# A decoder trunk on one Trainium2 core: the first stage's seven-product chunk set six units later, with its sums, its block fetches, the constants and the position terms moved

## The chip, the cores and the metric

The kernel runs on one core of one Trainium2 chip. The metric is the device time of one execution in microseconds (us), a median over several executions. PE is the matrix engine, DVE the vector engine, ACT the scalar engine, POOL the GpSimd engine and SP the sync engine, which here does nothing but issue DMAs. The page of the profile gives line numbers of kernel.py; L145 is a helper that records every call on PE, DVE and ACT, so rows are told apart by the names of their tiles, not by their lines.

## What is computed

Two layers of a decoder on 256 tokens of width 1024, all in float32. The change lies in the first half-step feed-forward block of layer 0, the first thing that the kernel does:

```python
def swiglu(x, w_gate, w_up, w_down):
    return (jax.nn.silu(x @ w_gate) * (x @ w_up)) @ w_down

# layer 0, first sub-layer; D_MODEL 1024, D_FF 2816, 256 tokens
hdn = swiglu(rmsnorm(x, ng[0]), ffn1_w_gate[0], ffn1_w_up[0], ffn1_w_down[0])
x = x + 0.5 * rmsnorm(hdn, ng[1])
```

The layer's mixer, which comes next, uses `compress_blocks`: blocks of 32 keys (or values), each with a position vector `pe` added, are multiplied by a weight `w1`. Since `(k + pe) @ w1` is `k @ w1` plus a term without tokens in it, the kernel works that constant term out once, ahead of the mixer. These are the position terms of the title.

```python
blk = k[:, idx] + pe[None, None, :, None, :]
return jax.nn.silu(blk.reshape(...) @ w1) @ w2
```

## The kernel before, in words

**Products in three parts.** Every weight is split into a high part `whi` (ACT casts it) and a low part `wlo` (DVE subtracts the high part from the raw weight), and the activations likewise into `xth` and `xtl`. One product is three matmuls: high by high, high by low, low by high. Each has a result of 128 tokens by 512 columns.

**Units.** The stage `f10` (`ffn`, L600, with `first=True`) streams its weights as units of 512 KB, a tile of 128 x 1024. They are counted here from 0, as the code counts them. Units 0 to 31 are four chunks of hidden columns (chunks 0, 1, 2 and 4 of 512 columns, eight units each, gate and up side by side). Units 32 to 35 are the last 256 columns, and units 36 to 49 are rows of the down weights. `unit` (L308) fetches a unit into a tile `raw` (a pool of 4 buffers), lets ACT write `whi` and DVE write `wlo`, and takes the buffers for these from two rings of six and four. `work` (L812) does the matmuls of one unit for one half of the tokens, t = 0 or t = 1: six matmuls for each. `lagged` (L565) runs over the units, t = 0 at once and t = 1 some units later, and calls what is registered for a unit: `at` ahead of it, `groups` behind it.

**Chunk ends.** After eight units the gate and up results of a token half stand in two PSUM banks. `chunk_end` (L607) multiplies: ACT writes silu of the gate into `sg`, DVE multiplies it by the up result, PE transposes it into `tp`, ACT and DVE split it into `hth` and `htl`. Only these reads by ACT and DVE free the two banks. The tiles `acc` share six banks.

**Seven products.** Hidden chunk 3 is computed by seven block products in place of eight (a scheme of Strassen's kind). `sums` (L674) first builds sums of the activation blocks in a tile `hx` (DVE), splits them into `sumh` and `suml` (ACT and DVE), and after that `hx` is free. The chunk's weight blocks come as eight transfers of 512 KB. Four go into a tile `wa` that is kept: `blocks` (L687) fetches two of them through SP at each of two units. Two are streamed through `raw` in phase one, which DVE also adds onto `wa`; two are streamed in phase six and added as well. The remaining sums of blocks are made by transfers that POOL issues and that accumulate onto `wa` in memory (`gather`, L699), four in number here. `wide_phases` (L758) gives the seven phases and a close, each run behind a given unit. A phase has twelve matmuls.

**Constants and position terms.** `tables` (L936) fetches two tables of 414 and 320 KB. `constants` (L942) fetches four small ones (`pv`, `pc`, `mu`, `small`). `compress_bias` (L963) fetches 1 MB of weights `cw`, multiplies them by the position vectors (four DVE operations of 128 x 512), adds them up in halves (ten DVE operations) and ends with two small matmuls into `tp` and a DVE operation that writes `cbias`.

**What sets the order.** A table, `GROUPS` (L38), says behind which unit each of these steps is recorded. Its row `False` serves this stage alone: `sums` at unit 7, blocks at units 13 and 14, phases behind units 16, 17, 18, 20, 21, 22, 23 and the close behind 24; the sums for the down weights at 30, the blocks of the down weights at 31 and 33. The tables are recorded at unit 11, the constants at 14, the position terms at units 24 to 33, in `wa[:, 0]`. The framework's scheduler then fixes the order on each engine, and each engine works through its own list in that order; SP's and POOL's transfers wait in their lists too. So a row that waits holds up all rows behind it on its engine.

Of the kernel before, what the change touches and what calls it, by code (L numbers as in the profile page):

```python
# [11 lines left out]
F32 = mybir.dt.float32  # L12
# [24 lines left out]
SEVEN = {True: (3, 4), False: (3,)}  # L37
GROUPS = {  # L38
    True: {"sums": 7, "down": 26, 3: (5, 6, (8, 9, 10, 12, 13, 14, 15, 16)), 4: (14, 16, (18, 19, 20, 22, 23, 24, 25, 26)), 0: (25, 26, (32, 33, 34, 35, 36, 37, 38))},
    False: {"sums": 7, "down": 30, 3: (13, 14, (16, 17, 18, 20, 21, 22, 23, 24)), 0: (31, 33, (39, 40, 41, 42, 43, 44, 45))},  # L40
}


# [133 lines left out]
class _Plan:  # L177
# [27 lines left out]
    def add(self, gen):  # L205
        self.strands.append(_Strand(gen))
# [16 lines left out]
class _Trunk:  # L223
# [376 lines left out]
    def ffn(self, units, gpost, last, kind, ahead=(), after=None, first=False, scale=None, following=None):  # L600

        nc, tc = self.nc, self.tc
# [251 lines left out]
        def lag(r):  # L854
            return min(LAG - 2 * (r == LAG - 1) - (LAG <= r < n - 8), max(8 - r if r < 8 else BASE, r + GROW - n))
# [4 lines left out]
        with tc.tile_pool(name="hp", bufs=1, reuse_waits="tile") as hp, self.work_pool():  # L860
            space = lambda dt: hp.tile([P, 2, 10, S], dt, name="hx", tag="hx")
            wa = hp.tile([P, 2, 2, D], F32, name="wa")
            at = {29: [], **({} if first else self.entry(self.scale_of(scale)))}
            add = lambda r, f: at.setdefault(r, []).append(f)
            between = {}
            for c in SEVEN[wide]:
                between.update(zip(groups[c][2], ([f] for f in wide_phases(c))))
            between.update(zip(groups[0][2], ([f] for f in down_phases())))
            add(groups["sums"], sums)
            add(groups["down"], down_sums)  # L870
            if first:
                self.begin(units, work, wa[:, 1].rearrange("p a b -> p (a b)")[:, 0:D])
                for r, f in ((4, lambda: self.stats_first(0)), (5, lambda: self.stats_first(1)), (11, self.tables), (14, self.constants),
                             *zip(range(24, 34), self.compress_bias(wa[:, 0]))):
                    add(r, f)
                pend = self.lagged(units, work, at, early, blocks, between, 3)
            else:
                pend = self.lagged(units, work, at, (lambda r: max(lag(r), r - n + 8)) if kind == "plain" else lag, blocks, between)
            rest = [lambda p=p: work(1, *p) for p in pend[:-2]]
            rest += [lambda p=p, h=h: work(1, *p, (h,)) for h in range(2) for p in pend[-2:]]  # L880
            if kind in ("mixer", "plain"):

                self.nc.scalar.activation(self.sm.tile([P, 2], F32, name="one", tag="st")[:, 0:1], htl[5].bitcast(F32)[:, 0, S - 1:S], AF.Exp)
            if kind in ("mixer", "plain"):
                self.rowsp = self.xp.tile([P, 2, D], F32, name="rows", tag="x8")
                for j, i in enumerate((gpost, last)[:1 if kind == "mixer" else 2]):
                    self.fetch(self.rowsp[:, j], self.rows[i].partition_broadcast(P), self.loads[-4])
                rows = [self.rowsp[:, j] for j in range(2)]
            else:
                row = self.xp.tile([P, 2, D], F32, name="rows", tag="x8")[:, 0]  # L890
                self.fetch(row, self.rows[gpost].partition_broadcast(P), self.loads[-4])
                rows = [row, None]
            self.finish(lambda t: [st[t, "y", 0], st[t, "y", 1]], rest, rows[0], True, kind, 2, ahead, rows[1], after, following)
# [69 lines left out]
    def compress_bias(self, w):  # L963

        nc = self.nc
        self.cbias = self.cp.tile([P, 1], F32, name="cbias")
        tile = []

        def load():
            tile.append(w.rearrange("p s (j e) -> p s j e", e=64))  # L970
            self.fetch(tile[0], self.cw[:, 0:2048].rearrange("p (s j e) -> p s j e", s=2, e=64), self.loads[-1])

        def scale(i, h):
            w = tile[0][:, i, 8 * h:8 * h + 8]
            o = 76 + 16 * i + 8 * h
            nc.vector.tensor_mul(w, w, self.pvt[:, o:o + 8, None].to_broadcast([P, 8, 64]))

        def add(i, n):
            w = tile[0][:, i]
            nc.vector.tensor_add(w[:, 0:n], w[:, 0:n], w[:, n:2 * n])  # L980

        def close():
            tp = self.tpp.tile([P, 4, P], F32, name="tp", tag="tp")
            for i in range(2):
                add(i, 1)
                nc.tensor.matmul(tp[64 * i:64 * i + 64, 0, 0:1], tile[0][:, i, 0], self.tabt[:, 767:768], start=True, stop=True)
            nc.vector.tensor_scalar(self.cbias, tp[:, 0, 0:1], 0.5, None, op0=ALU.mult)

        steps = [lambda i=i, h=h: scale(i, h) for i in range(2) for h in range(2)]
        return [load, *steps, *(lambda i=i: add(i, 8) for i in range(2)), lambda: (add(0, 4), add(1, 4)), lambda: (add(0, 2), add(1, 2)), close]  # L990
# [2011 lines left out]
```

## Time and profile before

| what | us |
|---|---|
| median of 3 runs | 1121.72 (1118.56 to 1121.87) |
| the profiled execution's own time | 1124.68 |
| its span, first to last instruction | 1122.9 |
| what lies around the span | 1.8 |
| PE busy in the span | 1100.0 (98%) |

The span is what every time on the page and in the trace counts from. A row of the timeline gives an instruction's start, its length, what it writes and reads, and in brackets how long its engine had been idle before it and what ended that. The granted clock is the share of full speed at which PE was run. The matmuls are pipelined: one shows 0.39 us, and the next starts 0.23 us behind it.

### The profile page before, as it was taken

What the parts mean: (1) busy time and instruction counts of PE and PEld (TensorE: products, weight loads), DVE (VectorE), ACT (ScalarE), POOL (GpSimd) and SP (SyncE); (2) the same over time, 40 slices, a digit from 0 to 9 for tenths busy, and PEclk for the clock granted to TensorE, in tenths of its full rate; (3) what the DMA queues carried; (4) which work ended last, traced back from release to release, by engine and by line L of the source; (5) the groups of instructions that cost most, each with busy time, mean ns of one, the idle gap of its engine ahead of it and who ended that gap; (6) DMA issues with size and microseconds to landing.
All of it is one profiled execution on the core that took longest, in us unless ns stands there. A gap on an engine that the chain in (4) does not pass through costs nothing.

```text
span 1122.9 us, 17815 instructions
## 1 busy us (share of the span) xinstructions
PE 1100.0 (98%) x6687; PEld 931.8 (83%) x6687; DVE 954.7 (85%) x1521; ACT 681.5 (61%) x1135; POOL 70.5 (6%) x122
## 2 busy tenths in 40 slices
PE   8999999999999999999999999999999999999997
PEld 6787888898988788888888888899989987888885
DVE  6878869889889999798898798886898798997985
ACT  5664656559866577665576666458514445775662
POOL 0010010000000011100010101000300000111000
PEclk9899999999999999999999999999999999999999
DMA  7877687453335588886668877732332324878870
GB/s 281 275 181 253 204 205 245 136 191 107 98 119 188 200 248 265 251 251 190 221 193 278 215 276 195 275 147 76 132 117 79 114 114 178 227 261 224 285 195 37
DMA packets 60854, 216.80 MB, mean 193 GB/s; under 512 B 7392, under 2 KB 7392, under 8 KB 60640
## 3 DMA queue, kind: packets, MB, share of 16 engines
q1 hardware_dynamic: 50400, 177.92, 45.6%
q0 software_dynamic: 10368, 37.75, 15.3%
q8 instruction: 52, 0.85, 0.3%
q14 instruction: 34, 0.28, 0.1%
HBM read 214.60 MB, written 1.05 MB: 192 GB/s over the span
## 4 chain that ended last, share of the span: by engine, by line
PE 81%; DVE 9%; ACT 4%; DMA 4%; issue 1%; SPq 0%; DVEq 0%; ACTq 0%
PE acc L145 77%; PE tp L145 4%; DMA raw<-in_wst_dram 4%; DVE wlo L145 3%; ACT whi L145 1%; DVE tm L145 1%; DVE tt L145 1%; DVE xtl L145 1%; ACT xth L145 1%; ACT junk L145 1%; ACT aT L145 0%; SPq L294 0%; ACT lc L145 0%; DVE x L145 0%; DMA xg<-in_x_dram 0%
## 5 line engine op out<-in xcount | busy, mean ns | idle before, releaser
L145 ACT CAST whi<-raw 128x1024 fp32r<-128x1024 f32 x239 | 246.4, 1054 | 123.5 <-DMA raw<-in_wst_dram 77.5
L145 DVE TENSOR_TENSOR wlo<-raw,whi 128x1024 fp32r<-128x1024 f32 x239 | 286.3, 1220 | 26.2 <-ACT whi L145 25.5
L145 PE MATMUL acc<-wlo,xth 128*128 128x512 f32 (+1 forms) x476 | 184.7, 391 | 1.0 <-DVE wlo L145 1.0
L145 PE MATMUL acc<-whi,xth 128*128 128x512 f32 (+1 forms) x476 | 180.3, 396 | 5.3 <-ACT sg L145 3.1
L145 PE MATMUL acc<-whi,xtl 128*128 128x512 f32 (+1 forms) x476 | 184.5, 391 | 0.4 <-DVE xtl L145 0.4
L145 ACT CAST whi<-wa 128x1024 fp32r<-128x1024 f32 (+1 forms) x112 | 115.2, 1044 | 68.3 <-DMA wa<-in_wst_dram 39.5
L145 DVE TENSOR_TENSOR wlo<-wa,whi 128x1024 fp32r<-128x1024 f32 (+1 forms) x112 | 133.5, 1209 | 19.0 <-ACT whi L145 18.9
L145 PEld LDWEIGHTS acc<-whi,xth 128*128 128x128 f32 x476 | 90.2, 190 | 25.3 <-ACT sg L145 4.3
L145 PEld LDWEIGHTS acc<-wlo,xth 128*128 128x128 f32 x476 | 90.1, 190 | 19.8 <-DVE wlo L145 2.5
L145 PEld LDWEIGHTS acc<-whi,xtl 128*128 128x128 f32 x476 | 90.3, 190 | 19.0 <-DVE xtl L145 0.9
L145 PE MATMUL acc<-whi,hx 128*128 128x512 f32 x320 | 104.2, 391 | 0.0
L145 PE MATMUL acc<-whi,xt 128*128 128x512 f32 x272 | 85.7, 391 | 0.0
L145 DVE TENSOR_TENSOR wa<-wa,raw 128x1024 f32<-128x1024 f32 x44 | 53.8, 1222 | 24.9 <-DMA raw<-in_wst_dram 22.3
L699 POOL DMA_DIRECT2D wa<-in_wst_dram x44 | 38.6, 877 | 555.0 <-DVE wlo L145 537.3
L145 PEld LDWEIGHTS acc<-whi,hx 128*128 128x128 f32 x320 | 60.0, 188 | 12.2
L145 PE MATMUL acc<-whi,sumh 128*128 128x512 f32 x176 | 69.3, 394 | 0.0
L145 PE MATMUL acc<-whi,suml 128*128 128x512 f32 x176 | 68.7, 390 | 0.0
L145 PE MATMUL acc<-wlo,sumh 128*128 128x512 f32 x176 | 68.6, 390 | 0.0
L145 PE MATMUL acc<-wlo,hx 128*128 128x512 f32 x160 | 62.5, 391 | 0.4 <-DVE wlo L145 0.4
L145 PEld LDWEIGHTS acc<-whi,xt 128*128 128x128 f32 x272 | 51.1, 188 | 10.5
L145 PE MATMUL acc<-wlo,xt 128*128 128x512 f32 x136 | 53.4, 393 | 0.2 <-DVE wlo L145 0.2
L145 PE MATMUL acc<-xnh,whi 128*128 128x256 f32 x160 | 46.3, 289 | 0.0
(436 smaller groups left out, 2213.6 us busy)
## 6 DMA issues: line engine op xcount, KB each, us to landing
raw<-in_wst_dram SPq DMA_DIRECT2D x256, 512.0 KB, 4.7
wa<-in_wst_dram POOLq DMA_DIRECT2D x72, 512.0 KB, 6.7
wa<-in_wst_dram SPq DMA_DIRECT2D x17, 512.0 KB, 7.0
lw<-in_wst_dram SPq DMA_DIRECT2D x12, 512.0 KB, 3.5
whi<-in_wst_dram SPq DMA_DIRECT2D x8, 512.0 KB, 5.8
wlo<-in_wst_dram SPq DMA_DIRECT2D x8, 512.0 KB, 5.0
wr<-in_wst_dram SPq DMA_DIRECT2D x8, 512.0 KB, 5.1
grow<-in_rows_dram SPq DMA_DIRECT2D x6, 512.0 KB, 5.7
```

Of the source, the lines that this page charges most:

```text
L145: r = f(out, *a, **k)
L699: nc.gpsimd.dma_start(home(i, p), place[key], accum_op=ALU.add)
```

## The change

Three edits, all for the stage `f10`:

1. In `GROUPS`, row `False`: the sums of chunk 3 are recorded at unit 14 in place of 7; its block fetches at units 18 and 19 in place of 13 and 14; its phases behind units 22, 23, 24, 26, 27, 28, 30 and the close behind 31. The sums for the down weights move from unit 30 to 32, and the second pair of the down weights' blocks from 33 to 32. The phases of the down weights stay.
2. The tables are recorded at unit 14 in place of 11, the constants at 16 in place of 14.
3. The position terms get a tile of their own, the first part of a new `hx` (the tile that the sums of chunk 3 had, and that the later results of the stage take), in place of `wa[:, 0]`, and are recorded at units 19 and 21 to 29 in place of 24 to 33. Their four multiplications are pinned: each has to stay behind the DVE operation recorded just before it.

```diff
@@ -37,7 +37,7 @@
-    False: {"sums": 7, "down": 30, 3: (13, 14, (16, 17, 18, 20, 21, 22, 23, 24)), 0: (31, 33, (39, 40, 41, 42, 43, 44, 45))},
+    False: {"sums": 14, "down": 32, 3: (18, 19, (22, 23, 24, 26, 27, 28, 30, 31)), 0: (31, 32, (39, 40, 41, 42, 43, 44, 45))},
@@ -870,8 +870,8 @@
-                for r, f in ((4, lambda: self.stats_first(0)), (5, lambda: self.stats_first(1)), (11, self.tables), (14, self.constants),
-                             *zip(range(24, 34), self.compress_bias(wa[:, 0]))):
+                for r, f in ((4, lambda: self.stats_first(0)), (5, lambda: self.stats_first(1)), (14, self.tables), (16, self.constants),
+                             *zip((19, 21, 22, 23, 24, 25, 26, 27, 28, 29), self.compress_bias(lambda: space(F32)[:, :, 0:4].rearrange("p s a b -> p s (a b)")))):
@@ -967,11 +967,12 @@
-            tile.append(w.rearrange("p s (j e) -> p s j e", e=64))
+            tile.append(w().rearrange("p s (j e) -> p s j e", e=64))
...
         def scale(i, h):
             w = tile[0][:, i, 8 * h:8 * h + 8]
+            nc.vector.pin = True
```

What this does to the lists of the engines. First place: SP, from unit 10 of the stage on. Before, `raw_415` is unit 10, `raw_437`, `raw_455` and `raw_473` are units 11 to 13 and `raw_512` is unit 14; `wa` are blocks of chunk 3.

```order
L294 DMA raw_415<-in_wst_dram 128x1024
L294 DMA tabs_433<-in_tabs_dram 128x828
L294 DMA tb_434<-in_tabs_dram 128x641
L294 DMA raw_437<-in_wst_dram 128x1024
L294 DMA raw_455<-in_wst_dram 128x1024
L294 DMA raw_473<-in_wst_dram 128x1024
L294 DMA wa_94<-in_wst_dram 128x1024 x2
L294 DMA pv_493<-in_pv_dram 128x108
L294 DMA pc_494<-in_pv_dram 128x32
L294 DMA mu_496<-in_pv_dram 128x48
L294 DMA small_495<-in_rows_dram 128x32
L294 DMA raw_512<-in_wst_dram 128x1024
```

The same place after, where `raw_402` is unit 10, `raw_456` unit 13, `raw_491` unit 14 and `raw_509` unit 15:

```order
L294 DMA raw_402<-in_wst_dram 128x1024
L294 DMA raw_420<-in_wst_dram 128x1024
L294 DMA raw_438<-in_wst_dram 128x1024
L294 DMA raw_456<-in_wst_dram 128x1024
L294 DMA tabs_487<-in_tabs_dram 128x828
L294 DMA tb_488<-in_tabs_dram 128x641
L294 DMA raw_491<-in_wst_dram 128x1024
L294 DMA raw_509<-in_wst_dram 128x1024
L294 DMA pv_539<-in_pv_dram 128x108
L294 DMA pc_540<-in_pv_dram 128x32
L294 DMA mu_542<-in_pv_dram 128x48
L294 DMA small_541<-in_rows_dram 128x32
```

Unit 14 now stands behind the two tables only; the four constants come behind unit 15, and the blocks `wa` behind units 18 and 19. The weights `cw` of the position terms come behind unit 21, where before they came behind unit 27.

Second place: DVE where the position terms are multiplied (`pv` holds the position vectors). Before, `wlo_913`, `wlo_954` and `wlo_975` are units 24 to 26.

```order
L145 TENSOR_TENSOR wlo_913<-raw_910,whi_912 128x1024
L145 TENSOR_TENSOR wlo_954<-raw_951,whi_953 128x1024
L145 TENSOR_TENSOR wa_94<-wa_94,pv_493 128x512 x4
L145 TENSOR_TENSOR formx_1049<-hth_547,htl_548 128x1024
L145 TENSOR_TENSOR wlo_975<-raw_972,whi_974 128x1024
```

After, where `wlo_672` and `wlo_691` are units 21 and 22 and `sg_521` is the product that ends chunk 1 for t = 0:

```order
L145 TENSOR_TENSOR wlo_672<-raw_669,whi_671 128x1024
L145 SCALAR_TENSOR_TENSOR sg_521<-acc_359,rs_y_242,sg_521 128x512
L145 TENSOR_TENSOR hx_628<-hx_628,pv_539 128x512 x2
L145 TENSOR_TENSOR hx_628<-hx_628 128x512
L145 TENSOR_TENSOR hx_628<-hx_628 128x256
L145 TENSOR_TENSOR wlo_691<-raw_688,whi_690 128x1024
```

Two of the four multiplications now stand ahead of unit 22; the other two stand further back, one at a time, between the subtractions of units 22 and 24.

Third place: DVE around phase six of chunk 3, whose two streamed blocks are added onto `wa`. Before, these are `raw_824` and `raw_837`; `wlo_727` is unit 20 and `wlo_768` unit 21.

```order
L145 TENSOR_TENSOR wlo_727<-raw_724,whi_726 128x1024
L145 TENSOR_TENSOR wlo_743<-wa_94,whi_742 128x1024
L145 TENSOR_TENSOR htl_548<-tp_549,hth_547 128x4x128
L145 TENSOR_TENSOR wlo_753<-wa_94,whi_752 128x1024
L145 TENSOR_TENSOR wa_94<-wa_94,raw_824 128x1024
L145 TENSOR_TENSOR htl_548<-tp_585,hth_547 128x4x128
L145 TENSOR_TENSOR wa_94<-wa_94,raw_837 128x1024
L145 TENSOR_TENSOR wlo_768<-raw_765,whi_767 128x1024
```

After, where the blocks are `raw_970` and `raw_983`, `wlo_869` is unit 26, `wlo_912` unit 27, and `sg_812` the product that ends chunk 2 for t = 1:

```order
L145 TENSOR_TENSOR wlo_869<-raw_866,whi_868 128x1024
L145 TENSOR_TENSOR wlo_885<-wa_94,whi_884 128x1024
L145 SCALAR_TENSOR_TENSOR sg_749<-acc_565,rs_y_242,sg_749 128x512
L145 TENSOR_TENSOR wa_94<-wa_94,raw_970 128x1024
L145 TENSOR_TENSOR wlo_895<-wa_94,whi_894 128x1024
L145 TENSOR_TENSOR wa_94<-wa_94,raw_983 128x1024
L145 SCALAR_TENSOR_TENSOR sg_812<-acc_601,rs_y_271,sg_812 128x512
L145 TENSOR_TENSOR wlo_912<-raw_909,whi_911 128x1024
```

A chunk's end, `sg_812`, now stands behind the addition of `raw_983`; before, the chunk ends nearest to these additions stood ahead of both. On PE the first matmuls for t = 1 of unit 8 now come behind the first matmul of unit 13, where before they came behind all of units 8 to 14 for t = 0. Behind this stage the lists of all engines are the same as before.

## The prediction

> **What bounds the kernel now.** I read the page first, then PE's busy time in stretches of 10 us over the stage that the change touches, then the timelines and the chain of waits around the two stretches that stand out. The page:
>
> ```profile
> span 1122.9 us, 17815 instructions
> ...
> PE 1100.0 (98%) x6687; PEld 931.8 (83%) x6687; DVE 954.7 (85%) x1521; ACT 681.5 (61%) x1135; POOL 70.5 (6%) x122
> ...
> PE 81%; DVE 9%; ACT 4%; DMA 4%; issue 1%; SPq 0%; DVEq 0%; ACTq 0%
> ```
>
> PE is busy for 98% of the span and carries most of the chain. The change adds and takes away no matmul, so it can only win PE's pauses, or make new ones. In stretches (columns: PE, PEld, DVE, ACT, POOL busy and count, granted clock, DMA share, GB/s):
>
> ```profile
> 30.00:40.00 10.00, 10.00 (x46) 8.29 (x45) 9.19 (x23) 6.51 (x11) 0.00 (x0) 1.00 0.81 266
> 40.00:50.00 10.00, 7.64 (x21) 5.00 (x21) 6.74 (x15) 6.42 (x7) 0.00 (x0) 0.71 0.82 313
> ...
> 100.00:110.00 10.00, 7.52 (x34) 5.90 (x33) 10.00 (x13) 4.98 (x7) 0.00 (x0) 1.00 0.41 112
> ```
>
> A full stretch starts about 46 matmuls. From 40 to 50 us there are 21, from 100 to 110 us 34. The first stretch also ran at a reduced clock; cut at the clock's own steps:
>
> ```profile
> 40.72:44.13 3.41, 1.70 (x7) 0.79 (x6) 1.78 (x6) 1.39 (x2) 0.00 (x0) 1.00 1.03 420
> 44.13:50.95 6.82, 6.17 (x15) 4.38 (x14) 5.28 (x8) 5.02 (x6) 0.00 (x0) 0.50 0.69 248
> ```
>
> PE's timeline at the first place. Between the first two rows lie 30 starts without a gap, 6.80 / 30 = 0.227 us each; then come three gaps, in the brackets:
>
> ```profile
> 33.93 0.39 PE L145 MATMUL acc<-whi,xtl 128*128 128x512 f32 x1
> ...
> 40.73 0.39 PE L145 MATMUL acc<-whi,xtl 128*128 128x512 f32 x1
> 42.30 0.73 PE L145 MATMUL acc<-whi,xth 128*128 128x512 f32 x2 [1.18 <-ACT whi L145]
> 43.56 0.50 PE L145 MATMUL acc<-wlo,xth 128*128 128x512 f32 x1 [0.53 <-DVE wlo L145]
> ...
> 45.82 0.80 PE L145 MATMUL acc<-whi,xth 128*128 128x512 f32 x1 [0.65 <-ACT sg L145]
> ```
>
> And at the second place one:
>
> ```profile
> 100.36 0.39 PE L145 MATMUL acc<-whi,xtl 128*128 128x512 f32 x1
> 103.23 0.50 PE L145 MATMUL acc<-whi,xth 128*128 128x512 f32 x1 [2.48 <-ACT sg L145]
> ```
>
> The chain of waits tells what lies behind each (start, length, what):
>
> ```profile
> 34.27 6.85 DMA raw<-in_wst_dram
> ...
> 41.20 1.05 ACT whi L145
> ...
> 42.28 1.23 DVE wlo L145
> ...
> 45.08 0.70 ACT sg L145
> ...
> 68.67 10.59 DMA raw<-in_wst_dram
> ...
> 94.77 6.68 DMA raw<-in_wst_dram
> ...
> 101.54 1.04 ACT whi L145
> 102.59 0.60 ACT sg L145
> ```
>
> At 34.27 SP issues unit 14; its cast is also what the first silu (`sg` at 45.08) stands behind on ACT, and PE needs that silu to get a bank back. At 94.77 it is one of the units behind the weights of the position terms, and again a silu stands behind its cast.
>
> **The first pause: 5.4 us, and what the change takes from it.** Gaps: 1.18 + 0.53 + 0.65 = 2.36 us. In the 6.82 us at clock 0.50 PE was busy for 6.17, of which half, 3.1 us, is lost. Together 5.4 us. Why unit 14 was late, on SP and DVE:
>
> ```profile
> 25.25 4.40 SPq L294 DMA_DIRECT2D raw<-in_wst_dram  x3
> 29.69 0.90 SPq L294 DMA_DIRECT2D wa<-in_wst_dram  x2
> ...
> 32.27 1.23 SPq L294 DMA_DIRECT2D mu<-in_pv_dram  x1
> 33.54 0.64 SPq L294 DMA_DIRECT2D small<-in_rows_dram  x1
> 34.27 0.48 SPq L294 DMA_DIRECT2D raw<-in_wst_dram  x1
> ```
>
> ```profile
> 21.83 1.22 DVE L145 TENSOR_TENSOR hx<-xth,xtl 128x1024 f32<-128x1024 f32 x1
> ...
> 26.93 1.22 DVE L145 TENSOR_TENSOR hx<-xth,xtl 128x1024 f32<-128x1024 f32 x1
> 28.07 1.22 DVE L145 TENSOR_TENSOR wlo<-raw,whi 128x1024 fp32r<-128x1024 f32 x1
> 29.53 1.23 DVE L145 TENSOR_TENSOR wlo<-raw,whi 128x1024 fp32r<-128x1024 f32 x1 [0.24 <-ACT whi L145]
> ```
>
> The last row is the subtraction of unit 10. It ends at 30.76 and frees the raw buffer that unit 14 takes. SP could have issued then; instead it worked through two blocks and four constants until 34.2, and the 1 MB of blocks also went ahead of unit 14 on the wire. In the changed list only the two tables stand between, 0.5 us each on SP, and they are out before 30.76. So unit 14 is issued by 30.8 at the latest. It may be earlier, by up to 2 us: unit 10 lands without the tables beside it, and of the sums' additions ahead of unit 9 one of about 1.1 us and one of 0.6 us are gone (the 21.83 and 26.93 rows are two, of which one now stands ahead of unit 8). Time to landing: 6.85 us from the row above as the worst, and in a quiet stretch of the same stage (110 to 140 us) this answer for `raw`:
>
> ```profile
> DMA to landing us min/median/max: 3.7/4.4/5.3
> ```
>
> Landing therefore lies between 28.8 + 4.4 = 33.2 and 30.8 + 6.85 = 37.65; I take 34.5, nearer to the quiet rows since there is only one unit and the tables on the wire. Behind it on ACT come the cast (1.05), a table load and the silu (0.70). The load, in ACT's timeline:
>
> ```profile
> 43.78 1.28 ACT L145 ACT_TABLE_LOAD   x1 [1.53 <-DVE rs_y L145]
> ```
>
> Before it stood 1.53 us for `rs_y`, which DVE finished behind unit 14's subtraction; in the changed list the `rs_y` of t = 0 is finished ahead of that subtraction, so this wait goes. The silu then ends about 3.1 us behind the landing, at 37.6 (36.3 to 40.8). PE wants its bank after the first of unit 13's six matmuls for t = 0. Those six end at 41.12 now (42.30 less 1.18); five of them at 0.227 make 1.1 us, so PE asks at 40.0. Margin 2.4 us, cost 0 to 0.8 us; I take 0. A gain below nothing is excluded here, since PE runs without a gap from 12 to 41 us and its matmuls stay. The 5.4 us are gone.
>
> **What the moved transfers cost.** Units 11 to 22, four blocks of `wa`, the 1 MB of `cw` and the tables are 12 x 0.52 + 4 x 0.52 + 1.05 + 0.75 = 10.2 MB from 24 us on. At 266 GB/s (the 30 to 40 row) they take 38 us and are in by 62; at the 420 GB/s of the 40.72 row 24 us, by 48. PE needs unit 22 after 131 matmuls and 16 transposes, at 40.0 + 131 x 0.227 + 16 x 0.11 = 71.5 (0.44 us for four transposes is a quarter more than three matmul starts, by the difference of starts around them). Even the slow end leaves 9 us for cast, subtraction and the position terms ahead of it on DVE. I take no pause. `cw` waits on SP for the sums' last subtraction, since it takes their `hx`: that ends, by the list, one subtraction behind unit 17's, near 46 us, while SP's next issue, unit 22, waits for unit 18's buffer until about 48. So it holds nothing up.
>
> **The second pause: 2.48 us.** DVE and SP behind it:
>
> ```profile
> 91.43 0.33 SPq L294 DMA_DIRECT2D wa<-in_cw_dram  x1
> 93.52 1.57 SPq L294 DMA_DIRECT2D raw<-in_wst_dram  x2
> ```
>
> ```profile
> 99.07 2.50 DVE L145 TENSOR_TENSOR wa<-wa,pv 128x512 f32<-128x512 f32 x4 [4.33 <-DMA wa<-in_cw_dram]
> ```
>
> `cw` went ahead of two units, and DVE stood 4.33 us for it with the subtractions of later units behind it. In the changed lists nothing of the position terms is left here. At their new place DVE may stand for `cw` as well: from 46.3, at 91.43 to 99.07 = 7.6 us, it is in at 53.9, and DVE gets there (behind unit 21 and `sg_521`) at about 54.7. Cost 0; if DVE stands 4.33 again, unit 22 is ready near 62 against 71.5, still 0. So 2.48 us are won.
>
> **The new place that is tight.** Unit 26 takes the ring buffer of phase one's first block, which PE leaves at 75.5 by the same count; with cast and subtraction (1.05 + 1.22) it frees a raw buffer at 77.8, and `raw_983` is issued. The addition (1.2) and `sg_812` (0.75) stand behind its landing. PE transposes `sg_812` after 209 matmuls and 20 transposes, at 89.6. With 4.4 us to land, `sg_812` is ready at 84.2; with the 10.59 us of the same transfer before (the 68.67 row; POOL's accumulating transfers ran beside it) at 90.3, 0.7 us late. I take 0, with 0.7 as the upper end. The rest of the chunk's waits were hidden before and keep their spacing from phase one to six.
>
> **Edits at nothing.** POOL no longer waits for the position terms, which now stand elsewhere:
>
> ```profile
> 142.09 1.19 POOL L696 DMA_DIRECT2D wa<-in_wst_dram  x2 [57.21 <-DVE cbias L145]
> ```
>
> PE had no gap there, so the wait cost nothing and its end brings nothing. The later sums for the down weights have the stretch of units 32 to 40 for cover, 20 us and more. Behind the stage all lists are the same; PE gets there earlier, and the transfers follow it since they wait for buffers that PE frees.
>
> **The sum.** 5.4 + 2.48 = 7.9 us less, with 0 to 1.5 us of it given back. On the profiled execution 1124.68 - 7.9 = 1116.8; on the median, which lies 2.96 below that execution, 1121.72 - 7.9 = 1113.8. About 0.3% (3.4 us) is what a measurement of this kernel can tell from no change.
>
> **Rivals.**
> *The clock falls anyway.* The halved clock is 3.1 of the 7.9. For its tie to the gaps speaks that it begins in a stretch of 3.41 us in which PE was busy for 1.70; against it, that one gap of 2.48 us at the second place left the clock at 1.00. If the fall isn't due to these gaps, it stays, and 4.8 us are won: 1116.9. The Trainium skill ("TensorE: Matmul & The Clock Gate", "Why this matters for your kernels") says that the clock drops when PE is idle for more than about 3 us at a stretch; by that the gaps here, 1.18 us at most, would not have done it. The trace differs from it: what it shows is half of a 3.41 us stretch idle in three gaps. So 0.08.
> *The second pause returns at the new place*, by `cw` or by the additions of phase six: 2.48 lost again, 1116.3. Against it speak 9 us of cover at unit 22; for it, the tight place. 0.08.
> *The first pause only moves.* If unit 14's silu comes so late that the three gaps and the clock come back, only the second pause is won: 1119.2, no change that can be told. It decides when unit 14 lands later than 37, which only the worst landing with the latest issue gives. 0.09.
> *Slower: DVE's waits meet.* Before, the additions of phase six stood for 1.66 + 2.03 us and the position terms for 4.33, some 20 us apart:
>
> ```profile
> 75.51 1.23 DVE L145 TENSOR_TENSOR wa<-wa,raw 128x1024 f32<-128x1024 f32 x1 [1.66 <-DMA raw<-in_wst_dram]
> ...
> 79.36 1.23 DVE L145 TENSOR_TENSOR wa<-wa,raw 128x1024 f32<-128x1024 f32 x1 [2.03 <-DMA raw<-in_wst_dram]
> ```
>
> Now all lie between units 21 and 27. If they used up the lead and came out on PE in full, that is 8.0 us, with the clock's 3.1 and the 0.8 of the first place 11.9: 1121.7 - 7.9 + 11.9 = 1125.7. It decides when DVE is more than 9 us behind at unit 22. 0.05. That the change doesn't do what it says isn't open: the lists show it.
>
> **The numbers.** Forecast 0.70, the others 0.08, 0.08, 0.09, 0.05. The forecast's own range is 1110.5 (the fastest run, 1118.56, less 7.9) to 1115.3. With the next two cases it reaches 1117.5 and holds 0.86, some of which I leave to the edges. Faster: 0.86; within 0.3%: 0.09; slower: 0.05.
>
> **What would show it.** PE without a gap over 0.3 us from 12 to 100 us and 45 or more matmuls in each stretch of 10 us; the granted clock at 1.00 from 40 to 55; unit 14 landing near 34.5 and the first silu ahead of 40; DVE's wait at `hx<-hx,pv` under 2 us; `sg_812` done ahead of 89.6. Wrong would be a gap on PE ended by `sg` near 40 or 90 us, or by DVE's `wlo` between 70 and 100, or a clock of 0.50 anywhere behind 11 us.

## The result and the profile after

Five runs of each kernel on one chip: before 1120.35 us (1118.53 to 1121.87), changed 1113.56 us (1112.17 to 1115.34). The ratio is 0.9941, with a 95% interval of 0.9922 to 0.9959, that is 4.6 to 8.7 us less. The forecast was 1113.8 us in 1110.5 to 1117.5. The profiled execution of the changed kernel took 1112.88 us, 11.8 us less than the one of before. The page:

```profile
span 1111.1 us, 17816 instructions
PE 1092.7 (98%) x6687; PEld 927.8 (84%) x6687; DVE 954.3 (86%) x1521; ACT 682.2 (61%) x1135; POOL 70.7 (6%) x122
PE 83%; DVE 9%; ACT 3%; DMA 2%; issue 2%; DVEq 0%; POOL 0%; ACTq 0%; POOLq 0%
```

The same stretches of 10 us as in the prediction (the columns are those of the tables there: length, busy time and count of PE, PEld, DVE, ACT, POOL, granted clock, DMA share, GB/s):

```profile
30.00:40.00 10.00, 10.00 (x46) 8.28 (x45) 9.37 (x24) 7.31 (x10) 0.00 (x0) 1.00 0.89 315
40.00:50.00 10.00, 10.00 (x49) 8.28 (x48) 9.14 (x12) 5.94 (x8) 0.00 (x0) 1.00 1.02 405
...
100.00:110.00 10.00, 10.00 (x47) 7.80 (x47) 10.00 (x12) 6.12 (x7) 1.07 (x2) 1.00 0.82 284
```

Where PE started 21 and 34 matmuls, it now starts 49 and 47, and the clock stays at 1.00. From 12 to 150 us the view of PE's waits has one row left (waiter, releaser, total, times, longest):

```profile
PE tp L145 <- DVE sg L145: 0.2, 1, 0.2
```

It lies where the prediction saw a tight place. The transfer of the first streamed block (`raw_970`) in the chain of waits, and behind it DVE up to the product that ends chunk 2 for t = 1:

```profile
75.14 8.84 DMA raw<-in_wst_dram
```

```profile
84.07 1.23 DVE L145 TENSOR_TENSOR wa<-wa,raw 128x1024 f32<-128x1024 f32 x1 [5.14 <-DMA raw<-in_wst_dram]
...
87.61 0.74 DVE L145 SCALAR_TENSOR_TENSOR sg<-acc,rs_y,sg 128x512 f32<-128x512 f32 x1
```

SP's issue of units 14 and 15, and the first silu, on ACT:

```profile
27.75 1.56 SPq L294 DMA_DIRECT2D raw<-in_wst_dram  x2
```

```profile
34.21 1.05 ACT L145 CAST whi<-raw 128x1024 fp32r<-128x1024 f32 x1 [2.06 <-DMA raw<-in_wst_dram]
35.27 1.28 ACT L145 ACT_TABLE_LOAD   x1
36.57 0.69 ACT L145 ACTIVATE sg<-acc,rs_y 128x512 f32<-128x512 f32 x1
```

Unit 14's cast starts 2.06 us after ACT ran dry, just when the unit lands. The table load follows without a wait for `rs_y`, and the silu ends at 37.26. PE's first matmul into the bank that it frees starts at 38.17 (37.94 plus one start of 0.227). The margin is 0.9 us.

**Where the 11.8 us between the two profiled executions lie**, by the start of the same matmul (the first is matmul 0): matmul 41 starts 1.65 us earlier (15.74 before, 14.09 after), matmul 620 9.84 us earlier (150.27 and 140.43). So the stretch that the change touches gave 8.2 us. The 1.65 us ahead of it are no work of the change; the same gap stands in both traces, ended by the same split of the activations, first before, then after:

```profile
11.66 0.73 PE L145 MATMUL acc<-whi,xtl 128*128 128x512 f32 x2 [0.42 <-DVE xtl L145]
```

```profile
10.04 0.73 PE L145 MATMUL acc<-whi,xtl 128*128 128x512 f32 x2 [0.43 <-DVE xtl L145]
```

In two more traces of the kernel before it ends at 10.14 and 11.59 us, so the unchanged kernel shows both values. The rest, 2.0 us, comes from behind the stage, where no list differs. The kernel before ran there for 3.41 us at half clock, which the changed kernel's execution did not, and which is 1.7 us of the 2.0 (from matmul 620 to the end the three traces of the kernel before took 970.5 to 972.6 us, the two of the changed kernel 970.7 and 974.6):

```profile
863.33:866.74 3.41, 2.86 (x95) 2.71 (x91) 2.21 (x7) 1.45 (x4) 0.00 (x0) 1.00 0.00 0
866.74:870.15 3.41, 3.41 (x33) 3.29 (x32) 0.85 (x3) 1.30 (x3) 0.00 (x0) 0.50 0.02 5
```

So this difference of two single executions overstates the change by 3.6 us.

### The profile page after: what moved, and what is told of

Read it like the earlier page. It is cut to its first block, busy times and chain, and to the rows that moved or that the text cites. A ratio compares the mean times of both kernels' runs of the same rounds, so it can differ in the third digit from the quotient of the medians.

```text
span 1111.1 us, 17816 instructions
## 1 busy us (share of the span) xinstructions
PE 1092.7 (98%) x6687; PEld 927.8 (84%) x6687; DVE 954.3 (86%) x1521; ACT 682.2 (61%) x1135; POOL 70.7 (6%) x122
## 4 chain that ended last, share of the span: by engine, by line
PE 83%; DVE 9%; ACT 3%; DMA 2%; issue 2%; DVEq 0%; POOL 0%; ACTq 0%; POOLq 0%
PE acc L145 79%; PE tp L145 4%; DVE wlo L145 2%; DMA raw<-in_wst_dram 2%; DVE tm L145 1%; DVE tt L145 1%; DVE xtl L145 1%; ACT xth L145 1%; ACT whi L145 1%; ACT junk L145 1%; ACT aT L145 0%; ACT lc L145 0%; DVE x L145 0%; DVE vm L145 0%; DVE formf L145 0%
```

## The experiments

| kernel | median, us | ratio to before (95%) | PE's gaps near 40 to 46 | near 89 | near 98 to 103 |
|---|---|---|---|---|---|
| changed, timed again | 1115.16 | 0.9951 (0.9935 to 0.9968) | none | 0.90 | none |
| blocks back | 1116.40 | 0.9961 (0.9947 to 0.9976) | none | 0.85 | 0.48 |
| constants back | 1117.27 | 0.9972 (0.9960 to 0.9985) | 0.90 | 0.96 | none |
| sums back | 1117.42 | 0.9977 (0.9964 to 0.9991) | 1.48 | none | none |
| before, constants alone | 1122.05 | 1.0015 (1.0002 to 1.0028) | 1.00 + 1.27 | none | 3.21 |
| before, terms alone | 1117.55 | 0.9978 (0.9965 to 0.9990) | 0.53 + 1.06 | none | none |
| before, silu first | 1120.08 | 0.9996 (0.9981 to 1.0012) | 2.95 | none | 0.64 |
| terms late | 1114.03 | 0.9948 (0.9934 to 0.9963) | none | none | none |
| phase six later | 1114.00 | 0.9948 (0.9933 to 0.9964) | none | none | none |
| both late | 1113.42 | 0.9937 (0.9918 to 0.9956) | none | none | none |

The kernel before had medians of 1119.56, 1119.98 and 1120.10 us beside these runs. Gaps are those over 0.12 us in the one trace of each kernel.

**The changed kernel again.** No edit.

> The changed kernel as it is, timed again on this chip as the measure for the other runs. Theory (two pauses of PE are gone, 5.4 and 2.5 us): about 7 us less than the kernel before, PE without a gap over 0.3 us from 12 to 100 us except at the product that ends chunk 2 for t = 1 (0.2 us in the first trace), granted clock 1.00 from 40 to 55 us. Rival (part of the first difference was luck of one profile): a gap or a clock of 0.50 shows up again in this stage, and the gain is under 5 us.

The ratio means 5.5 us less (3.6 to 7.3). There is no gap in the stage but the one near 89 us, here 0.90:

```profile
89.42 0.66 PE L145 MATMUL tp<-ident,sg 128*128 128x128 f32 x4 [0.90 <-DVE sg L145]
```

Ahead of the program's end the clock fell once, far behind the stage (at 715.5 us). So theory and rival each have a part: the pauses are gone in both traces, and the size of the first difference was partly luck.

**Blocks back.** Is it the blocks of chunk 3 ahead of unit 14?

```diff
-    3: (18, 19, (22, 23, 24, 26, 27, 28, 30, 31))
+    3: (13, 14, (22, 23, 24, 26, 27, 28, 30, 31))
```

> The changed kernel with the first block fetches of chunk 3 back at units 13 and 14, so that two blocks stand ahead of unit 14 on SP again. Theory 1 (what cost time was the blocks and constants ahead of unit 14): unit 14 lands at 37 us or later in place of 34.1, the first silu ends past 40, PE has gaps of 2 us or more near 38 to 42 and the clock may fall: 1116 to 1120 us. Theory 2 (what counts is where the first silu stands on ACT; in this list it stands ahead of the cast of unit 14): unit 14 is as late as under theory 1, but the silu doesn't wait for it, PE asks for unit 14 only near 46 us, and there is no gap: 1113.6 us, as the changed kernel.

Unit 14 lands at 36.87 in place of 34.13, and PE has no gap near 40. (The gap of 0.48 us at 103 us is another wait, ended by DVE's `u`.) ACT shows why (the silu stands ahead of the late unit's cast):

```profile
35.57 1.28 ACT L145 ACT_TABLE_LOAD   x1 [3.04 <-DVE rs_a L145]
36.87 0.69 ACT L145 ACTIVATE sg<-acc,rs_y 128x512 f32<-128x512 f32 x1
37.74 1.06 ACT L145 CAST sumh<-hx 128x1024 fp32r<-128x1024 f32 x1 [0.18 <-DVE hx L145]
38.70 1.05 ACT L145 CAST whi<-raw 128x1024 fp32r<-128x1024 f32 x1
```

Theory 2 is right here: a late unit costs nothing as long as the silu isn't behind it. In time the two kernels can't be told apart (0.9961 and 0.9951).

**Constants alone.** The kernel before with edit 2 only.

```diff
-    (11, self.tables), (14, self.constants)
+    (14, self.tables), (16, self.constants)
```

> The kernel before with edit 2 alone: tables at unit 14, constants at unit 16. Unit 14 still stands behind two blocks and now the tables on SP, but no longer behind the four small constants; the first silu stands behind its cast as before. Theory: unit 14 is issued near 32.3 in place of 34.3 us and lands near 39; PE's gaps at 41 to 46 us shrink from 2.4 to between 0 and 1.5 us; with under 1 us of gap the clock stays at 1.00, and 3 to 5 us are won (1115.5 to 1117.5), otherwise about 1 us. The second pause stays at 2.5 us. Rival (the blocks on the wire alone make unit 14 late): it lands near 41 again and the time is that of the kernel before, 1120.

The rival is right. SP issued unit 14 at 31.00 in place of 34.27, and it landed at 40.53, hardly earlier than before (41.12). The chain:

```profile
31.00 9.53 DMA raw<-in_wst_dram
...
41.67 1.28 ACT L145
...
42.97 0.70 ACT sg L145
```

SP's 3.3 us only became 2.7 us more of transfer: two blocks were on the wire ahead of it, and by this edit the two tables as well. Which of the two held it the run doesn't tell. The gaps at 41 to 46 us sum to 2.27 us, as against 2.36. The second pause came out at 3.21 us, and with 1122.05 us the kernel is no faster than before, if anything 0.2% slower.

**Constants back.** The same step from the other side: the changed kernel without edit 2.

```diff
-    (14, self.tables), (16, self.constants)
+    (11, self.tables), (14, self.constants)
```

> The changed kernel with edit 2 undone: tables at unit 11, constants at unit 14. Unit 14 stands behind four small constants on SP again, and in this list the first silu stands on ACT behind the casts of units 14 and 15. Theory 1 (SP's time for the constants delays the silu): unit 14 lands near 35.5 and unit 15 near 37 us, the silu ends near 40, PE asks for its bank near 38.8: a gap of about 1.2 us, 1115 us, and up to 3.4 more where the clock falls to 0.50. Theory 2 (only the blocks on the wire delayed units there): unit 14 lands near 34 as in the changed kernel, no gap, 1113.8.

Unit 14 lands at 34.28, as theory 2 had it, but unit 15 at 36.74, as theory 1 had it. The silu stands behind both casts and ends at 39.88, and PE loses 0.90 us, so theory 1 is right in what counts:

```profile
36.82 1.05 ACT L145 CAST whi<-raw 128x1024 fp32r<-128x1024 f32 x1 [1.41 <-DMA raw<-in_wst_dram]
37.89 1.28 ACT L145 ACT_TABLE_LOAD   x1
39.19 0.69 ACT L145 ACTIVATE sg<-acc,rs_y 128x512 f32<-128x512 f32 x1
```

```profile
39.92 0.50 PE L145 MATMUL acc<-whi,xth 128*128 128x512 f32 x1 [0.90 <-ACT sg L145]
```

So edit 2 is worth something only together with the rest of the change: alone it gained nothing, and its undoing brings a gap back.

**Sums back.** The changed kernel with the sums at unit 7.

```diff
-    False: {"sums": 14, "down": 32,
+    False: {"sums": 7, "down": 32,
```

> The changed kernel with the sums of chunk 3 back at unit 7, ahead of the subtractions of units 7 to 12 on DVE. Blocks and constants stay where the change puts them. Theory 1 (the blocks ahead of unit 14 were the cause of the first pause): unit 14 lands by 36 us, no gap near 40: 1113.8. Theory 2 (what counts is when the last cast ahead of the first silu on ACT is ready; in this list the silu stands behind the casts of units 14 to 17): unit 17 is issued when unit 13's subtraction ends, near 37, lands near 41.6, the silu ends near 44.7, while PE asks for its bank near 43: a gap of 1 to 2.5 us, 1115 to 1116.5, and 1.7 or 3.4 more where the clock falls.

Theory 2 again, with its numbers: unit 14 lands early (35.82), but the silu stands behind the casts up to unit 17. The chain shows that unit in transfer, its cast, the table load, the silu, and PE:

```profile
35.13 5.63 DMA raw<-in_wst_dram
40.83 1.05 ACT whi L145
41.90 1.28 ACT L145
43.20 0.70 ACT sg L145
43.94 5.76 PE acc L145 x24
```

The gap is 1.48 us. By the ratios, the kernel with the constants back and this one lie 2.4 and 2.9 us above the changed kernel timed again (with intervals that overlap a little), which is more than their gaps; from matmul 41 to 620 their traces took 128.49 and 127.83 us, as against 126.35 and 126.92. What the rest is due to is not shown.

**Silu first.** If the cast ahead of the silu is all, forbidding that order in the kernel before should help. (`CAST` is 16, the count at the cast of unit 14.)

```diff
+    silu = nc.scalar.activation(sg[:, :n], gate, AF.Silu, scale=r)
...
+    if self.casts == CAST and self.silu:
+        self.tc.add_manual_dep(r.ins, self.silu, info, reason="silu")
```

> The kernel before with one thing more: the cast of unit 14 on ACT has to stay behind the first silu. SP's list is that of before, so unit 14 is as late as before; DVE's list differs in two rows, and PE now takes the matmuls of unit 8 for t = 1 straight behind unit 13, and unit 14 some 36 matmuls later. Theory 2 (the first pause is the silu standing behind a cast whose unit is late): the silu waits only for rs_y, which DVE has near 40.6 us, and ends near 42.6; PE asks at 41.1 on the clock of before: one gap of about 1.5 us in place of 1.18 + 0.53 + 0.65, no stretch with half of PE's time idle, so no fall of the clock: 1117 to 1119. Theory 1 (the late unit 14 itself is what PE lacks): the gaps and the time of before, 1120. The second pause stays in both.

It did not: 0.9996, and one gap of 2.95 us. On ACT the table load, free of the cast, waits for `rs_y`; on DVE `rs_y` stands behind the subtractions of the sums (`suml`):

```profile
40.56 1.28 ACT L146 ACT_TABLE_LOAD   x1 [2.20 <-DVE rs_y L146]
41.85 0.69 ACT L146 ACTIVATE sg<-acc,rs_y 128x512 f32<-128x512 f32 x1
```

```profile
38.87 1.22 DVE L146 TENSOR_TENSOR suml<-hx,sumh 128x1024 fp32r<-128x1024 f32 x1
...
40.33 0.15 DVE L146 SCALAR_TENSOR_TENSOR rs_y<-rs_a,rs_y 128x1 f32<-128x1 f32 x1
```

(The helper's line is 146 in this kernel.) The last step of `rs_y` behind that row ends at 40.48, and PE had asked at 39.6 (42.59 less 2.95), six matmuls earlier than in the list of before. So theory 2 was too narrow: the silu had two late predecessors in the kernel before, the cast of a late unit on ACT and `rs_y` on DVE. A second execution of the kernel before (described below) shows the second one by itself. There unit 14 landed at 38.60 and its cast ended at 39.73, but the silu still waited for `rs_y`, which stands behind unit 14's subtraction, and that behind the sums' subtraction:

```profile
41.88 1.28 ACT L145 ACT_TABLE_LOAD   x1 [2.14 <-DVE rs_y L145]
```

```profile
39.05 1.22 DVE L145 TENSOR_TENSOR suml<-hx,sumh 128x1024 fp32r<-128x1024 f32 x1
...
40.38 1.22 DVE L145 TENSOR_TENSOR wlo<-raw,whi 128x1024 fp32r<-128x1024 f32 x1
...
41.64 0.15 DVE L145 SCALAR_TENSOR_TENSOR rs_y<-rs_a,rs_y 128x1 f32<-128x1 f32 x1
```

In all three traces of the kernel before, `rs_y` came last of the two, and the silu stood for it for 1.53, 2.14 and 1.53 us. In the changed kernel the sums' splits stand behind the silu, so both are gone. The sums alone, or the blocks alone, were not moved in the kernel before.

**Terms alone.** The kernel before with the position terms in the new region, at units 16 to 22.

```diff
-    *zip(range(24, 34), self.compress_bias(wa[:, 0]))
+    *zip((16, 17, 18, 18, 19, 19, 20, 20, 21, 22), self.compress_bias(lambda: space(F32)...))
```

> The kernel before with edit 3 alone, as far as it goes there: the position terms in a region of their own and earlier, here at units 16 to 22, since chunk 3 needs that region back at unit 23. Theory (the two pauses are independent): the second pause near 101 us goes, the three gaps at 41 to 46 us and the clock of 0.50 stay: 2.5 us won, 1117.9. Rival (the pause only moves): the 1 MB of weights, now ahead of phase one's additions, makes DVE stand there, a gap of about 2.5 us shows up on PE between 55 and 75 us, and the time is that of the kernel before, 1120.

2.5 us (0.9978, 1.1 to 3.9 us) is what the theory gave. The second pause is gone, the first stays, with the clock at half for one stretch behind it:

```profile
40.78 0.50 PE L145 MATMUL acc<-wlo,xth 128*128 128x512 f32 x1 [0.53 <-DVE wlo L145]
43.04 0.61 PE L145 MATMUL acc<-whi,xth 128*128 128x512 f32 x1 [1.06 <-ACT sg L145]
```

```profile
39.87:43.29 3.42, 1.83 (x7) 0.93 (x6) 1.99 (x8) 2.28 (x3) 0.00 (x0) 1.00 1.02 419
43.29:46.70 3.41, 3.41 (x9) 2.63 (x9) 3.23 (x4) 3.10 (x4) 0.00 (x0) 0.50 1.07 411
```

**Terms late.** The prediction's slower rival, provoked.

```diff
-    *zip((19, 21, 22, 23, 24, 25, 26, 27, 28, 29), self.compress_bias(...))
+    *zip((25, 26, 26, 27, 27, 28, 28, 29, 29, 29), self.compress_bias(...))
```

> The changed kernel with the position terms later: their weights fetched at unit 25, the products and sums at units 26 to 29, among the additions of phase six, still in the region of their own. This is the rival of the prediction in which DVE's waits meet. Rival: DVE stands for the weights, and the 1 MB delays the streamed blocks, so the product that ends chunk 2 for t = 1 comes 1.5 us or more later than in the changed kernel, PE's gap near 89 us (0.2 and 0.9 us in the two traces of the changed kernel) grows to 2 to 4 us, and the time is 1116 to 1119. Theory that the cover is enough: the gap stays under 1 us and the time is 1113.8.

The rival falls. DVE doesn't stand for the weights. It waits for the streamed block 1.54 us in place of 5.14, the subtraction that stood between the two additions stands ahead of both in this list, the product is done in time, and PE has no gap at all from 12 to 150 us:

```profile
84.37 1.23 DVE L145 TENSOR_TENSOR wa<-wa,raw 128x1024 f32<-128x1024 f32 x1 [1.54 <-DMA raw<-in_wst_dram]
```

**Phase six later, and both.** Two versions without the gap near 89 us.

```diff
-    (22, 23, 24, 26, 27, 28, 30, 31)
+    (22, 23, 24, 26, 28, 30, 31, 32)
```

> The changed kernel with the phases of chunk 3 behind units 22, 23, 24, 26, 28, 30, 31, 32: five, six, seven and the close later. The product that ends chunk 2 for t = 1 then stands ahead of both additions of phase six on DVE. Theory (the gap near 89 us comes from the addition that waits for its block): the gap goes, DVE's wait of 5 us for the block stands behind that product and is hidden, 0.2 to 0.9 us less than the changed kernel, which the time will hardly show. Rival (the later phases push something else late): a new gap between 95 and 125 us, 1 us or more slower.

The second has this and the later terms.

> The changed kernel with the later position terms and the later phases of the two kernels that had no gap over 0.3 us between 12 and 130 us. Theory (all pauses of PE in this stage are then gone in every execution): no gap over 0.3 us there, 0.2 to 0.9 us less than the changed kernel, about 1113, which the measurement can't tell from it. Rival (both push work late, and together something shows): a gap of 1 us or more between 85 and 130 us.

Neither has a gap over 0.12 us between 12 and 150 us. The theory of the gap (the product stands behind an addition that waits for its block) holds. 1114.00 and 1113.42 us can't be told from the changed kernel (1113.56 and 1115.16), as was expected.

**The kernel before, twice more, for the clock.** No edit.

> The kernel before once more, for its trace. Theory (the granted clock is set anew each 3.41 us, and falls to 0.50 for the next 3.41 us when PE started some 8 matmuls or fewer in that time, of 15 possible): the gaps at 41 to 46 and at 101 to 103 us come back at nearly the same size (about 2.4 and 2.5 us), but how much clock they cost (0, 1.7 or 3.4 us each) depends on how the 3.41 us windows fall on them in this execution. Rival (the clock falls whenever the gaps are there): 3.4 us behind the first pause again and none behind the second.

> The same kernel a third time, with the same two expectations: by the windows, gaps of nearly the same size with another loss to the clock; by the rival, the same loss of 3.4 us behind the first pause.

Gaps at the first place 0.18 + 1.14 + 1.06 and 0.70 + 0.52 + 1.06 us, at the second 1.32 and 2.69, so there one is half of the 2.5 expected; no loss to the clock at either place, in either execution. The rival falls. The windows of 3.41 us, laid through the clock's own steps in each execution, around the first place and the second, of the second execution and of the third:

```profile
39.88:43.29 3.41, 1.83 (x6) 0.87 (x6) 2.58 (x10) 1.40 (x2) 0.00 (x0) 1.00 1.00 388
43.29:46.71 3.42, 2.80 (x12) 2.31 (x13) 2.63 (x4) 3.42 (x5) 0.00 (x0) 1.00 0.50 189
94.50:97.91 3.41, 2.09 (x10) 1.41 (x8) 3.41 (x5) 2.83 (x4) 0.00 (x0) 1.00 0.17 71
```

```profile
41.21:44.63 3.42, 1.93 (x6) 0.97 (x6) 2.08 (x7) 1.87 (x3) 0.00 (x0) 1.00 1.06 414
44.63:48.04 3.41, 2.80 (x12) 2.34 (x13) 2.64 (x4) 3.41 (x5) 0.00 (x0) 1.00 0.46 179
95.83:99.24 3.41, 1.96 (x9) 1.30 (x7) 2.91 (x5) 1.49 (x2) 0.00 (x0) 1.00 0.25 102
```

Six starts in a window did not bring the clock down here, so the count of eight in the expectation was the wrong measure. PE's busy time in the window orders the cases of this stage: see the last section.

## Why the prediction was right, and where it was luck

**The first pause is gone: right.** Unit 14 was issued at 27.75 (expected 28.8 to 30.8), landed at 34.13 (34.5), the silu ended at 37.26 (37.6). PE asked at 38.2, not 40.0, since this execution's stage began 1.65 us earlier, so the margin was 0.9 us and not 2.4. With these 1.65 us added, unit 14 landed and the silu ended 1.3 us later than forecast: the issue was in time (29.4), but the transfer took 6.38 us, near the 6.85 that stood for the worst. That 34.13 fits 34.5 is luck.

**The reason given was only part of it.** The prediction said that unit 14 was late because SP worked through two blocks and four constants, and because the blocks were on the wire. The constants alone in the kernel before gained nothing. Blocks back in the changed kernel cost no gap near 40: the scheduler then put the silu ahead of the late cast. And with the silu put ahead in the kernel before, it still waited 2.20 us for `rs_y`. What the change did at this place is two things together: the sums' splits went behind the silu on DVE and ACT, and the last cast ahead of the silu is of a unit that SP issues at 27.75 in place of 34.27. Undoing the sums alone gives 1.48 us of gap, undoing the constants alone 0.90. The prediction treated `rs_y` in one sentence and put it down to unit 14's subtraction, with which it was to go. But it was a bound of its own: behind the sums it was ready only at 40.48 even where nothing tied it to unit 14 (silu first), and the prediction counted the sums only as a little of unit 14's issue time.

**The second pause is gone: right.** Terms alone gain 2.5 us. In the changed kernel DVE goes through the products without a wait:

```profile
53.98 1.29 DVE L145 TENSOR_TENSOR hx<-hx,pv 128x512 f32<-128x512 f32 x2
```

The prediction had put it at 54.7, with the weights landed at 53.9. They landed at 53.89, 0.1 us before DVE asked for them, so the wait of nothing was close.

**The tight place: right in place, a little over in size.** 0.23 and 0.90 us in two traces, against 0 taken and 0.7 as the upper end. The second is a sign that the prediction had named as wrong (a gap ended by `sg` near 90 us). It needed slow landings. For `raw` from 60 to 90 us of the changed kernel the trace answers:

```profile
DMA to landing us min/median/max: 3.4/4.3/9.7
```

The longest is `raw_983`, nearer to the worst row (10.59) than to the quiet ones (4.4) that I took. But the prediction looked at this block alone: in the trace the chain of waits runs through the first one, `raw_970` (8.84 us, landed at 83.98), its addition and a subtraction, and `raw_983` had landed 0.26 us before its own addition began.

**The sum: right in the profiled execution, mis-sized for the median.** Forecast 7.9 us, measured 8.2 in the stage between the two traces. But the term of 3.1 us for the halved clock belongs to that one execution. In the three traces of the kernel before the gaps are 4.84, 3.70 and 4.97 us, on average 4.50, and the loss to the clock in the stage 3.1, 0 and 0. From matmul 41 to 620 these executions took 134.53, 130.65 and 131.89 us, the two of the changed kernel 126.35 and 126.92: 5.7 us less on average.

The other runs say the same, since each one's mean granted clock is on record. It is 0.9968 on average in the 62 runs of the kernel before beside the experiments (0.995 at the lowest), 0.9982 in the eleven of the changed kernel, and 0.994 in the execution that the prediction read. As an estimate, the missing share of the clock times the span is 3.55 us on average before and 2.02 after, which makes the clock term 1.5 us over the whole program. With it the sum is 4.50, less 0.57 for the gap that is left in the changed kernel (mean of 0.23 and 0.90), and 1.5: 5.5 us, beside the measured 6.6 (4.6 to 8.7) and 5.5 (3.6 to 7.3).

The rival "the clock falls anyway" priced the case of no clock term at 4.8 us. That is nearer to the second measurement than 7.9, but not by its mechanism: the falls in this stage do follow windows with the gaps in them. The forecast of 1113.8 came out within 0.3 us also because the median that it started from, 1121.72 of three runs, lay above those of the larger samples, 1119.56 to 1120.35. That is luck. (Two slips change nothing: the lower edge of the range, 1118.56 less 7.9, is 1110.7 and not 1110.5, and 0.44 us for four transposes is about two matmul starts, not over three; the counts use the 0.44.)

**The rivals.** The slower one (DVE's waits meet) did not happen, and did not when provoked. The return of the second pause happened in no trace. A first pause that only moves happened where the sums or the constants were undone.

## What to carry to other kernels

An instruction that frees a bank starts behind its last predecessor, so list all of them (the cast ahead of it on its engine, the scale that another engine computes, the table load) with the time at which each is ready, before naming one as the cause: here two were late, and removing one of them, the cast, gained nothing. Ask of a loss in one profiled execution whether it would be there in the next: gaps that follow from the order came back in three executions, the halved clock behind them in one. And compare a span or a difference of two traces stage by stage, since 3.6 of the 11.8 us lay where nothing had changed.

## What the runs showed of the hardware

**The granted clock changes on a fixed grid of 3.41 us, and with products of 128 x 512 it follows how busy PE was in the window before.** Every fall ahead of the program's end lasts 3.41 or 6.83 us, and falls lie on a grid: in the kernel before, the one at 866.74 comes 241 windows behind the one at 44.13 (822.61 / 3.413 = 241.0). PE's busy time by the profile in a window at full clock, and the clock in the next:

| window | PE busy, us | clock in the next |
|---|---|---|
| silu first, 38.83 | 0.81 | 0.50 |
| constants alone, 96.28 | 0.86 | 0.50 |
| changed again, 712.13 | 1.54 | 0.50 |
| before, 40.71 | 1.71 | 0.50 |
| terms alone, 39.87 | 1.83 | 0.50 |
| before, second execution, 39.88 | 1.83 | 1.00 |
| before, third execution, 41.21 | 1.93 | 1.00 |
| before, third execution, 95.83 | 1.96 | 1.00 |
| before, 98.74 | 2.01 | 1.00 |

In these windows, with products of 128 x 512, the step lies near 1.83 of 3.41 us, 54%. Of the windows that are themselves at 0.50, two with 2.75 and 2.76 us busy were followed by another at 0.50, those with 3.07 us or more by 1.00. So how long the pauses are doesn't settle what they cost: 1.59 us (terms alone) and 2.95 (silu first) cost one window at half clock, 2.36 (before) and 3.21 (constants alone) two, and 2.28 to 2.69 us at other places and in other executions of the kernel before none, by how the grid falls on them. The Trainium skill ("TensorE: Matmul & The Clock Gate", "What's actually happening") gives a free-running window of 3413 ns, with which the grid agrees; it calls the condition an idle window, and here windows with PE busy for 0.81 to 1.83 us of 3.41 were enough.

The windows of the kernel with the constants alone show a whole fall, with a pause of 3.21 us (97.14 to 100.35) where it starts:

```profile
96.28:99.69 3.41, 0.86 (x4) 0.38 (x2) 3.38 (x5) 2.07 (x3) 0.00 (x0) 1.00 0.35 142
99.69:103.10 3.41, 2.75 (x7) 2.17 (x8) 3.41 (x5) 1.19 (x3) 0.00 (x0) 0.50 0.28 78
103.10:106.52 3.42, 3.42 (x10) 2.65 (x9) 3.42 (x5) 1.67 (x2) 0.00 (x0) 0.50 0.68 224
```

**The step is not one of busy time alone.** In the mixer, with products of 64 x 32 and 64 x 64, a window with PE busy for 2.86 us was followed by one at 0.50 (863.33 above). Near 825 us, where transposes and products of 128 x 160 and 128 x 512 are mixed, windows with 1.45 to 1.50 us busy were followed by 0.50 in four kernels (sums back, silu first, terms late, phase six later) and windows with 1.48 to 1.59 by 1.00 in three (changed, blocks back, both late). What the chip counts there stays open; no run here tells it.
